# A two-layer hybrid backbone: z read behind the spill branch and gated on POOL, the latents' norm first, all z products ahead of the scans, and the second MoE's scale and shift on gathered rows

## The chip, the cores and the metric

The kernel runs on one core of one Trainium2 chip. A core has TensorE (PE in the profile, with its weight loads as PEld), VectorE (DVE), ScalarE (ACT), GpSimd (POOL) and SyncE (SP, which issues most DMAs here). Each engine works through its own queue of instructions in order. The metric is the device time of one execution in microseconds, the median of several runs.

## The reference

256 latent tokens and 256 context tokens of width 1024 go through two layers. Each layer has a mixer and a mixture of experts (MoE); each of these has its own norm, with scale, shift and gate from a conditioning vector. Layer 0 mixes by a gated convolution and differential attention, layer 1 ("odd") by a recurrent block. The layer-1 context is only needed up to its last scan state.

```python
h  = modulate(rms_norm(x, norm_mix[l]), sh1, sc1)        # h * (1 + scale) + shift
x  = x + g1 * mixer(h, hc)
hf = modulate(rms_norm(x, norm_ffn[l]), sh2, sc2)
x  = x + g2 * hier_moe(hf, ...)                          # the group's best, then two experts of its 4

# odd mixer, per direction (forward and reverse), u = second half of z = h @ w_in, y = gelu(first half)
uc = depthwise_conv(u, conv_w, conv_b)                   # four taps
r, i = sigmoid(block_diag(uc, w_a) + b_a), sigmoid(block_diag(uc, w_x) + b_x)
log_a = -8 * r * softplus(-lam)
a, b = exp(log_a), sqrt(-expm1(2 * log_a)) * (i * uc)
h_t = a_t * h_{t-1} + b_t                                # context first; the latents start from its end
y_lat = (y * (h_forward + h_backward)) @ w_out
```

Each token goes to 2 of 16 experts of width 512, and all is float32. The answer is the latent stream, 256 x 1024.

## The kernel before, in words

**Memory and order.** Working memory is 23 units of 128x2048 float32 (8 KB a partition) and some smaller pieces. Python code hands units out from one queue: `unit()` takes the one given back longest ago, `give()` puts one at the end. A weight tile of 1 MB fills a unit; the list `todo` holds the order of the weight loads, and `load_ahead(n)` keeps up to n loaded tiles ahead. So the place of a `give()` in the source sets which later tile or load gets that unit, and hence on whose work it waits. The source order gives the priority; the instructions are laid out on each engine by priority among those that a planner of the compiler holds to be ready, so their order isn't quite that of the source. `tc.issue_after(x)` puts an instruction behind x on its engine.

**Numbers.** Products that feed the routing are done with each operand as a high and a low part (`split`, L152: a copy on ACT, L155, and a subtraction, L158) in three matmuls (`mm3`, L176). MoE products use the operands as they are.

**First MoE (`moe0`, L1081).** The experts are done in four quarters of four. A quarter has 3 row blocks, in each of which every expert has 32 token rows. `four` (L1058) runs the four experts' 32-column products beside each other (L1066). The rows come by indirect DMA; the outputs of the first three quarters are scattered by indirect DMA into a DRAM tensor z with two places for each token (L1106). Rows of z that an over-full expert didn't write are zeroed by `empty()` in the second quarter, 8 indirect DMAs on POOL. The last quarter's outputs stay on chip and are added by one-hot products (`add`, L1234). Behind its up product, z is read by 8 DMAs on SP (L1213) into four units, the gate rows by two (L437); then comes `spill_rounds` (L973), a branch on the number of extra rounds, taken by all five engines (L980). Its body runs only when an expert got over 96 tokens (64 in layer 1), and the branch skipped it in these runs. Then POOL adds the two halves of z (L1223), DVE multiplies by the gate (L1224) and adds to the residual x (L1225), and `between` splits the first u weight (subtractions on DVE) and adds the first half of the last quarter: `add_gated` (L550: L554 times gate, L555 plus residual), squares and their sums on ACT (L1240).

**The odd mixer's norm (`second_T`, L516).** For the latents (s = 0), then the context (s = 1): the second half of the last quarter is added (`ready`), the root of the mean square is taken, x is normed (L529), transposed (L481), scaled (L544, L545) and split. Both `ready` calls come ahead of any transposes. `ada(1, 1)` (L366) makes the second MoE's scale and shift on PE (L391) among it.

**The odd mixer (`odd_mixer`, L1395).** Channels go in four groups i of 256. `z(i)`: split the weight u_i, 96 matmuls for both streams. `conv(i)`: a first tap on ACT (L1444), three on DVE (L1446), for both directions and halves. `gate(i)`: 8 matmuls (L1459), 8 sigmoids on ACT, a multiply on POOL (L1461). `tanhs`, `exps`, `roots`: on ACT by `table` (L1412), which chains all such calls in source order, since a change of function needs a table load (all L1415). `exps` has a step on DVE (L1476). `scan(i)`: multiply, scan, add (L1487, L1488, L1491). `yrows(i)`: the y product (L1499), `gelu`, `mix(i)` (L1508), and `outs(i)` (L1519), the output product. The order is written by hand (L1524 to L1574): z(3) comes behind scan(0) and scan(1).

**Second MoE (`moe1`, L1266).** `moe_norm` (L765) takes the logits from the raw residual by scaled router weights, and writes normed rows with scale and shift (L795, and L796 half on POOL); `in_parts` splits them (L158). `route` (L830) is a chain of some 45 small DVE operations; `rows_of` (L1048) makes one-hots S, and `gather` (L1285) picks rows by a product (L1293). Four quarters follow, with two row blocks.

Of the kernel before, what the change touches and what calls it, by code (L numbers as in the profile page):

```python
# [17 lines left out]
D = 1024  # L18
KD = 8
# [16 lines left out]
def backbone(ctx: ExitStack, tc: tile.TileContext, a: dict, out: bass.AP):  # L36
# [329 lines left out]
    def ada(l, g, late=False, tag="z"):  # L366
# [6 lines left out]
        def biases():  # L373
            r = piece([128, 512], "vectors")
            V.memset(r, 0.0)
# [140 lines left out]
    def second_T(ready, between):  # L516
# [5 lines left out]
        def over_rms(s, sq):  # L522
# [5 lines left out]
            for b in range(2):  # L528
                V.tensor_scalar(xn[:, b], xb(2 * s + b), r[:, b:b + 1], None, op0=ALU.mult)  # L529
            return xn  # L530

        for s in range(2):
            if s == 0:
                xn = over_rms(0, ready(0))
                sq = ready(1)
                between()
            else:
                xn = over_rms(1, sq)
                give(xt[1])
# [433 lines left out]
    def spill_rounds(l, cap, nb, load, key, w, nri):  # L973
# [6 lines left out]
        with tc.If(n > 0):  # L980
# [7 lines left out]
            V.memset(y, 0.0)  # L988
            cur = slot1.rearrange("p a b -> p (a b)")
            V.tensor_scalar(cur, slot0, float(cap), None, op0=ALU.add)  # L990
            with tc.For_i(0, n, 1):
                with tc.For_i(0, NE, 1) as e:
# [6 lines left out]
                    gather_slots(hgT, h2, Sl)  # L999
                    t = act_of(*[slots_by(hgT, [dyn(a[m][l, bass.ds(e, 1)])], KD, keep) for m in ("wg", "wu")])  # L1000
# [80 lines left out]
    def moe0(h2, ts, lg, rest, h2d):  # L1081
# [31 lines left out]
        def empty():  # L1113
# [6 lines left out]
            for i in range(2):  # L1120
                for b in range(NT):
                    scatter(rowi[:, i, b:b + 1], zero)
# [55 lines left out]
        for q in range(4):  # L1178
# [15 lines left out]
            if q == 1:  # L1194
                empty()
# [12 lines left out]
        zt = z.rearrange("(i b p) d -> i b p d", i=2, p=128)  # L1208
        zs = []
        for b in range(NT):  # L1210
            zs.append(unit([128, 2, D], "zb"))
            for i in range(2):
                nc.sync.dma_start(zs[b][:, i], zt[i, b])  # L1213
        gates = gate_rows(0, 5, 2)
        spill_rounds(0, CAP0, NT, again, key, w, nri)
# [6 lines left out]
        for b in range(NT):  # L1222
            G.tensor_add(zs[b][:, 0], zs[b][:, 0], zs[b][:, 1])  # L1223
            V.tensor_mul(zs[b][:, 0], zs[b][:, 0], gates[:, b // 2])  # L1224
            V.tensor_add(xb(b), xb(b), zs[b][:, 0])  # L1225
            give(zs[b])
# [7 lines left out]
        def add(h, b):  # L1234
# [4 lines left out]
            add_gated(b, h, p, gates[:, b // 2])  # L1239
# [17 lines left out]
        def ready(s):  # L1257
            for b in (2 * s, 2 * s + 1):
                add(1, b)
# [6 lines left out]
    def moe1(h2, ts, lg, rest):  # L1266
        nb = 2
        load_ahead(13)

        hp = [unit([128, 2, D], "hp", R) for _ in range(2)]  # L1270

        def in_parts(b):
            for i in range(2):
                c = slice(512 * i, 512 * i + 512)
                split(hp[0][:, b, c], hp[1][:, b, c], h2[b][:, c], V)

        in_parts(0)
        goh, ef, pos, key, w, nri = route(nb, lg, CAP1)
        rest()
        in_parts(1)  # L1280
        give(*ts)
        ks = view(small([128, 16], "ks"), [128, 2, nb])
        hgT = unit([128, KD, 256], "hgT")

        def gather(q):  # L1285
            S = piece([128, nb, 256], "S", R)
            rows_of(S, key, nb, q, range(NR1), ks)
            for k in range(0, KD, 2):
                p = bank([128, 2, 256])
                for i in range(2):  # L1290
                    for b in range(nb):
                        for m, h in enumerate(hp):
                            T.matmul(p[:, i], h[:, b, (k + i) * 128:(k + i + 1) * 128], S[:, b],  # L1293
                                     start=(b + m == 0), stop=(b + m == nb))
                evict(hgT[:, k:k + 2], p)

        gather(0)
# [26 lines left out]
        for q in range(4):  # L1324
# [15 lines left out]
            if q == 3:  # L1340
                spill_rounds(1, CAP1, nb, whole, key, w, nri)
# [53 lines left out]
    def odd_mixer(ready, wz):  # L1395
# [144 lines left out]
        exps(0)  # L1540
        exps(1)
# [151 lines left out]
```

## Time and profile before the change

| | us |
|---|---|
| median of 3 runs | 1043.9 |
| lowest and highest | 1042.34, 1045.82 |
| profiled execution | 1043.87 |
| its span in the profile | 1042.1 |

| engine | busy us | share of the span |
|---|---|---|
| PE | 953.0 | 91% |
| DVE | 430.3 | 41% |
| ACT | 282.0 | 27% |
| POOL | 133.3 | 13% |

The profile is of one execution. A line of a group has the source line, engine, operation and tile, then busy time, mean ns of one, and the idle time ahead of them with what ended it. A line of the timeline has start and length in us, the engine (SPq is SP's queue, PEldq PE's sequencer), the operation, and in brackets how long the engine was idle before it and for what. A busy PE can be a PE that runs at a lower clock: the granted clock stands beside it, 1.00 being full.

### The profile page before, as it was taken

The page shows a single profiled execution, that of the slowest core. Times are in us where ns is not written, and L with a number is a line of the kernel's source. Part 1 is how long each engine was busy: PE and PEld are TensorE (multiplying, and loading weights), DVE is VectorE, ACT ScalarE, POOL GpSimd, SP SyncE. Part 2 cuts the span into 40 slices and gives each one's busy share as a digit, 9 for nine tenths or more (in the row PEclk, how much of TensorE's full clock was granted, in tenths as well). Part 3 has the DMA queues.
Part 4 walks back from the last instruction along what each step waited for, and adds up shares of the span by engine and source line. Part 5 has one row for each costly group of instructions (what it writes and reads, how often), then busy time and mean ns, then how long its engine had stood idle before and what let it go on. Part 6 is the DMA issues. An engine that isn't in the chain of part 4 may idle for free. (4 is left out here: it accounts for less than half of the span.)

```text
span 1042.1 us, 16137 instructions
## 1 busy us (share of the span) xinstructions
PE 953.0 (91%) x6705; PEld 523.3 (50%) x6705; DVE 430.3 (41%) x946; ACT 282.0 (27%) x494; POOL 133.3 (13%) x117
## 2 busy tenths in 40 slices
PE   4699999999987999999999799995986899999987
PEld 2488756656876343343433246873644443434323
DVE  3756666666464020020101188748667321111102
ACT  3623333424121010010100036486862110001000
POOL 0254010121033211010010300212121000000000
PEclk9699999999997999999999899996997899999999
DMA  9932466779476699999999946220793499999994
GB/s 366 372 111 100 162 236 256 298 295 419 198 294 242 258 391 393 421 409 414 420 361 380 390 189 270 99 104 17 291 357 148 158 422 420 421 419 420 421 388 196
DMA packets 50705, 310.73 MB, mean 298 GB/s; under 512 B 8680, under 2 KB 9448, under 8 KB 16064
## 3 DMA queue, kind: packets, MB, share of 16 engines
q1 hardware_dynamic: 45648, 301.63, 72.9%
q0 software_dynamic: 4976, 7.99, 2.1%
q8 instruction: 55, 0.90, 0.3%
q14 instruction: 26, 0.21, 0.1%
HBM read 304.28 MB, written 13.70 MB: 305 GB/s over the span
## 5 line engine op out<-in xcount | busy, mean ns | idle before, releaser
L1066 PE MATMUL ba<-w,hgT 128*32 128x512 f32 x1536 | 181.3, 593 | 1.6 <-SPq L980 0.9
L1066 PEld LDWEIGHTS ba<-w,hgT 128*32 128x32 f32 x1536 | 55.7, 110 | 114.6 <-issue 109.2
L1066 PE MATMUL ba<-w,actT 128*32 128x512 f32 x800 | 95.2, 593 | 1.9 <-DVEq L980 1.1
L178 PE MATMUL bz<-hT,wsp 128*128 128x256 f32 (+1 forms) x224 | 77.6, 347 | 6.4 <-ACT wsp L155 6.4
L180 PE MATMUL bz<-hT,wsp 128*128 128x256 f32 (+1 forms) x224 | 75.2, 336 | 4.3 <-DVE wsp L158 4.3
L179 PE MATMUL bz<-hT,wsp 128*128 128x256 f32 (+1 forms) x224 | 75.2, 336 | 0.0
L1066 PEld LDWEIGHTS ba<-w,actT 128*32 128x32 f32 x800 | 33.9, 110 | 55.8 <-issue 50.8
L1066 PE MATMUL bz<-w,actT 128*32 128x512 f32 x480 | 56.0, 605 | 6.0 <-PEq L980 5.9
L1066 PE MATMUL bz<-w,hgT 128*32 128x512 f32 x512 | 60.5, 592 | 0.0
L155 ACT ACTIVATE wsp<-w 128x512 fp32r<-128x512 f32 (+1 forms) x60 | 42.7, 765 | 51.7 <-PE bz L180 18.0
L158 DVE TENSOR_TENSOR wsp<-w,wsp 128x512 fp32r<-128x512 f32 (+1 forms) x53 | 49.0, 958 | 10.3 <-ACT wsp L155 10.2
L178 PEld LDWEIGHTS bz<-hT,wsp 128*128 128x128 f32 x224 | 43.0, 192 | 15.3 <-ACT wsp L155 10.5
L180 PEld LDWEIGHTS bz<-hT,wsp 128*128 128x128 f32 x224 | 43.0, 192 | 9.8 <-DVE wsp L158 6.1
L179 PEld LDWEIGHTS bz<-hT,wsp 128*128 128x128 f32 x224 | 43.2, 193 | 3.0 <-issue 0.2
L1334 DVE SCALAR_TENSOR_TENSOR act<-ba,tg,silu 128x512 f32<-128x512 f32 x8 | 6.0, 751 | 90.1 <-PE ba L1066 90.1
L391 PE MATMUL bz<-w,sT 128*32 128x512 f32 x320 | 39.5, 612 | 3.8 <-DMA w<-in_ada_w_dram 3.8
L179 PE MATMUL bz<-wsp,hT 128*128 128x512 f32 x96 | 38.8, 405 | 3.4 <-DVE wsp L158 3.4
L1446 DVE SCALAR_TENSOR_TENSOR uc<-bz,ocw,uc 128x510 f32<-128x510 f32 (+2 forms) x48 | 34.4, 743 | 15.7 <-ACT uc L1444 15.1
L178 PE MATMUL bz<-wsp,hT 128*128 128x512 f32 x96 | 38.3, 405 | 2.4 <-ACT hT L155 2.4
L1461 POOL TENSOR_TENSOR uc<-uc,ii 128x512 f32<-128x512 f32 x16 | 25.8, 1626 | 104.4 <-ACT ii L1415 104.4
L1190 DVE SCALAR_TENSOR_TENSOR act<-ba,tg,silu 128x512 f32<-128x512 f32 x6 | 4.5, 752 | 83.5 <-PE ba L1066 83.5
L180 PE MATMUL bz<-wsp,hT 128*128 128x512 f32 x96 | 38.5, 401 | 0.0
(363 smaller groups left out, 1488.6 us busy)
## 6 DMA issues: line engine op xcount, KB each, us to landing
w<-in_wg_dram SPq DMA_DIRECT2D x64, 1024.0 KB, 12.2
w<-in_wu_dram SPq DMA_DIRECT2D x64, 1024.0 KB, 11.1
w<-in_wd_dram SPq DMA_DIRECT2D x64, 1024.0 KB, 10.7
w<-in_ada_w_dram SPq DMA_DIRECT2D x48, 1024.0 KB, 8.0
w<-in_od_w_in_dram SPq DMA_DIRECT2D x8, 1024.0 KB, 7.0
w<-in_w_qkv_dram SPq DMA_DIRECT2D x6, 1024.0 KB, 19.9
w<-in_w_conv_dram SPq DMA_DIRECT2D x6, 1024.0 KB
w<-in_ev_w_out_dram SPq DMA_DIRECT2D x4, 1024.0 KB
```

The lines of the kernel that those rows point to most:

```text
L155: S.activation(hi, src, AF.Copy)
L158: (eng or lo_engine()).tensor_sub(lo, src, hi.bitcast(F))
L178: T.matmul(o, l[0], r[0], start=start, stop=False)
L179: T.matmul(o, l[0], r[1], start=False, stop=False)
L180: final[0] = T.matmul(o, l[1], r[0], start=False, stop=stop)
L391: T.matmul(m[32 * j:32 * j + 32], sT[:, k], w[:, j * 512:(j + 1) * 512], start=(k == 0), stop=(k == KD - 1), tile_position=(0, 32 * j))
L1066: T.matmul(o[r][32 * j:32 * j + 32], rows(r, k0 + k)[:, 32 * j:32 * j + 32], ws[j][:, k], start=(k0 + k == 0), stop=(k0 + k == nk - 1), ti ...
L1190: V.scalar_tensor_tensor(act[r], u[r], tg[:, n:n + 1], sl[r], op0=ALU.mult, op1=ALU.mult)
L1334: V.scalar_tensor_tensor(act[r], u[r], tg[:, n:n + 1], sl[r], op0=ALU.mult, op1=ALU.mult)
L1446: V.scalar_tensor_tensor(c[:, :, j:256], src[:, :, 0:256 - j], tap, c[:, :, j:256], op0=ALU.mult, op1=ALU.add)
L1461: G.tensor_mul(uc[:, n], uc[:, n], ii)
```

## The change

1. **Order of loads.** u1, u2, u3 come first, then y0 to y3; before, y0 and y1 came between u2 and u3.
2. **z.** `empty` moves into the spill branch's body. The z reads (four of 1 MB) and the gate rows come behind the branch in the source, the gate rows first. z is multiplied by the gate on POOL. Its addition to x stays on DVE, behind the first half's gated adds, and its units are given back only there. The u weight is split with subtractions on POOL, behind those adds.
3. **The latents' norm first.** The context's gated adds of the second half are put behind the latents' last normed block on DVE.
4. **Order of the odd mixer.** z(3) and conv(3) come ahead of the scans.
5. **Second MoE.** The raw rows, divided by their root mean square, are gathered as two parts (a copy with scale on ACT, a difference on DVE), and scale and shift are applied per channel when the gathered, transposed rows are evicted. The tiles of scale and shift rows and the split go.

```diff
     for i in range(1, 4):
         w_rows(("u", i), a["od_w_in"][4 + i])
-        if i == 2:
-            for j in range(2):
-                w_rows(("y", j), a["od_w_in"][j])
-    for i in range(2, 4):
+    for i in range(4):
         w_rows(("y", i), a["od_w_in"][i])
...
-            V.memset(r, 0.0)
+            (G if late else V).memset(r, 0.0)
...
             if s == 0:
-                xn = over_rms(0, ready(0))
-                sq = ready(1)
+                xn, done = over_rms(0, ready(0))
+                sq = ready(1, done)
                 between()
...
-    def spill_rounds(l, cap, nb, load, key, w, nri):
+    def spill_rounds(l, cap, nb, load, key, w, nri, empty=lambda zeros: None, ab=None):
...
             V.memset(y, 0.0)
+            empty(y)
...
                     gather_slots(hgT, h2, Sl)
+                    for k in range(KD if ab else 0):
+                        V.tensor_scalar(hgT[:, k], hgT[:, k], ab[0][k], ab[1][k], op0=ALU.mult, op1=ALU.add)
...
-            if q == 1:
-                empty()
...
-        zt = z.rearrange("(i b p) d -> i b p d", i=2, p=128)
+        spill_rounds(0, CAP0, NT, again, key, w, nri, empty)
+        gates = gate_rows(0, 5, 2)
+        zt = z.rearrange("(i b p) d -> b p i d", i=2, p=128)
         zs = []
         for b in range(NT):
             zs.append(unit([128, 2, D], "zb"))
-            for i in range(2):
-                nc.sync.dma_start(zs[b][:, i], zt[i, b])
-        gates = gate_rows(0, 5, 2)
-        spill_rounds(0, CAP0, NT, again, key, w, nri)
+            nc.sync.dma_start(zs[b], zt[b])
...
             G.tensor_add(zs[b][:, 0], zs[b][:, 0], zs[b][:, 1])
-            V.tensor_mul(zs[b][:, 0], zs[b][:, 0], gates[:, b // 2])
-            V.tensor_add(xb(b), xb(b), zs[b][:, 0])
-            give(zs[b])
+            G.tensor_mul(zs[b][:, 0], zs[b][:, 0], gates[:, b // 2])
...
-            add_gated(b, h, p, gates[:, b // 2])
+            with tc.issue_after(after.ins) if after else nullcontext():
+                add_gated(b, h, p, gates[:, b // 2])
...
             if r == 0:
-                w = wtile(("u", 0))
-                wz.extend(split_cols(w, m, V) for m in range(2))
-                used(w)
                 for b in range(NT):
                     add(0, b)
+                for b in range(NT):
+                    V.tensor_add(xb(b), xb(b), zs[b][:, 0])
+                    give(zs[b])
+                    square(0, b)
+                w = wtile(("u", 0))
+                wz.extend(split_cols(w, m, G) for m in range(2))
+                used(w)
...
-        def ready(s):
+        def ready(s, after=None):
             for b in (2 * s, 2 * s + 1):
-                add(1, b)
+                add(1, b, after)
+                square(1, b)
```

The second MoE's gather, and the order of the odd mixer:

```diff
-                evict(hgT[:, k:k + 2], p)
+                V.tensor_scalar(hgT[:, k], p[:, 0], ab[0][k], ab[1][k], op0=ALU.mult, op1=ALU.add)
+                S.activation(hgT[:, k + 1], p[:, 1], AF.Identity, scale=ab[0][k + 1], bias=ab[1][k + 1])
...
-        load_ahead(13)
+        load_ahead(15)
...
         z(2)
+        conv(2)
         gate(1)
-        conv(2)
+        z(3)
+        give(*tiles[0], *tiles[1])
         tanhs(0)
         tanhs(1)
+        exps(0)
+        exps(1)
         gy = unit([128, KD, 256], "gy")
         mixT = unit([128, KD, 256], "mixT")
         yrows(0)
         yrows(1)
-        exps(0)
-        exps(1)
         roots(0)
         roots(1)
+        conv(3)
+        load_ahead(4)
         scan(0)
         scan(1)
-        z(3)
-        give(*tiles[0], *tiles[1])
         gelu(0)
         mix(0)
         mix(1)
         gate(2)
-        conv(3)
-        yrows(2)
         tanhs(2)
         exps(2)
+        yrows(2)
+        yrows(3)
+        give(whole)
         roots(2)
+        scan(2)
         gate(3)
         give(*wax)
-        yrows(3)
-        give(whole)
-        scan(2)
         tanhs(3)
...
-        step, *tokens = moe_norm(2, "a", *AB)
...
+            V.scalar_tensor_tensor(lg[:, b], lp, r, rc[:, 0], op0=ALU.mult, op1=ALU.add)
+            S.activation(hp[0][:, b], xb(b), AF.Copy, scale=r)
+
+            def low(b=b, r=r):
+                V.scalar_tensor_tensor(hp[1][:, b], xb(b), r, hp[0][:, b].bitcast(F), op0=ALU.mult, op1=ALU.subtract)
+
+            if b == 0:
+                low()
```

`low` of the second token block (b = 1) is handed to `gather(0)`, which issues it behind its one-hots.

More of the change, by code (lines that the diff above doesn't have):

```diff
@@ L1111, in scatter, with empty @@
             puts.append(st)
-        def empty():
+        def empty(zeros):
             row = small([128, 2, NT], "row")
@@ L1121, in empty @@
                 for b in range(NT):
-                    scatter(rowi[:, i, b:b + 1], zero)
+                    scatter(rowi[:, i, b:b + 1], zeros)
         def again():
@@ L1232, in put, with add @@
                 put_parts((yl[r][:, 0, hs], yl[r][:, 1, hs]), o[r])
-        def add(h, b):
+        def add(h, b, after=None):
             p = bank([128, 512])
@@ L1264, in moe0, with moe1, gather @@
         return ready, wz
-    def moe1(h2, ts, lg, rest):
+    def moe1(hp, lg, low):
         nb = 2
-        load_ahead(13)
[L1270 to L1277, printed above, removed]
+        load_ahead(15)
         goh, ef, pos, key, w, nri = route(nb, lg, CAP1)
-        rest()
-        in_parts(1)
-        give(*ts)
         ks = view(small([128, 16], "ks"), [128, 2, nb])
         hgT = unit([128, KD, 256], "hgT")
-        def gather(q):
-            S = piece([128, nb, 256], "S", R)
-            rows_of(S, key, nb, q, range(NR1), ks)
+        ab = [[t[1][:, 0, k:k + 1] for k in range(KD)] for t in (AT, BT)]
+        def gather(q, then=lambda: None):
+            S_ = piece([128, nb, 256], "S", R)
+            rows_of(S_, key, nb, q, range(NR1), ks)
+            then()
             for k in range(0, KD, 2):
@@ L1576, in odd_mixer @@
         g1 = gate_rows(1, 2, 1)
-        AB = moe_rows(1, 1), router(1, 1, "a")
+        parts = router(1, 1, "a")
+        hp = [unit([128, 2, D], "hp", R) for _ in range(2)]
         load_ahead(12)
-        step, *tokens = moe_norm(2, "a", *AB)
         outs(3, ((0, 0), (1, 0), (0, 1), (1, 1)))
@@ L1583, in odd_mixer @@
         load_ahead()
+        wa, rc = parts
+        lg = small([128, 2, 20], "lg")
+        sq = small([128, NT, 2], "sq_sums")
+        lows = []
         for b in range(2):
+            xT = []
+            lp = None
             for h in range(2):
                 add_gated(b, h, y[b][h], g1[:, 0])
-            step(b)
+                S.activation(piece([128, 512], "sq", BF), xb(b)[:, h * 512:(h + 1) * 512], AF.Square,
+                             accum_out=sq[:, b, h:h + 1])
+                p = bank([128, 4, 128])
+                for c in range(4):
+                    T.transpose(p[:, c], xb(b)[:, (4 * h + c) * 128:(4 * h + c + 1) * 128], ident)
+                xT.append(piece([128, 4, 128], "x2T"))
+                evict(xT[-1], p)
+            lp = bank([128, 20])
+            for c in range(KD):
+                T.matmul(lp, xT[c // 4][:, c % 4], wa[0][:, c], start=(c == 0), stop=(c == KD - 1))
+            ss = small([128, 1], f"ss{b}")
+            V.tensor_add(ss, sq[:, b, 0:1], sq[:, b, 1:2])
+            r = small([128, 1], f"rstd{b}")
+            rsqrt(r, ss, float(D), [128, 1], f"m{b}")
+            V.scalar_tensor_tensor(lg[:, b], lp, r, rc[:, 0], op0=ALU.mult, op1=ALU.add)
[4 more added lines that the diff above has]
+                low()
         give(g1)
-        return tokens
+        return hp, lg, low
     xT = first_norm()
```

20 lines of the change are left out of this document (10 added, 10 removed).

## The prediction

> **What bounds the kernel now.** I read the page first: its span and the rows of 40 slices, of 26 us each.
>
> ```profile
> span 1042.1 us, 16137 instructions
> PE   4699999999987999999999799995986899999987
> ...
> DMA  9932466779476699999999946220793499999994
> ```
>
> PE is busy nearly everywhere. The slices in which it isn't, after the start, are 22, 27, 29 and 30 (counted from 0): some 573 to 807 us. The DMA engines are full from slice 32 to the end but one, and have holes in the same stretch of 573 to 807 us. That is the second half of the first mixture of experts (MoE), the odd mixer, and the way into the second MoE. So I asked for busy times stage by stage there (columns: stretch, then its length; PE, weight loads, DVE, ACT, POOL; clock; DMA share; GB/s).
>
> ```profile
> 582.00:649.00 67.00, 57.98 (x428) 31.83 (x430) 42.32 (x75) 25.45 (x54) 9.06 (x6) 0.95 0.71 281
> 649.00:687.00 38.00, 38.00 (x235) 29.54 (x235) 27.83 (x44) 19.56 (x29) 8.73 (x7) 1.00 0.32 112
> 687.00:714.00 27.00, 23.37 (x121) 19.11 (x119) 12.95 (x18) 26.53 (x41) 1.84 (x2) 0.99 0.12 39
> 714.00:737.00 23.00, 14.25 (x60) 10.31 (x61) 20.27 (x26) 9.98 (x16) 6.47 (x3) 0.63 0.32 104
> 737.00:770.00 33.00, 32.73 (x107) 20.04 (x107) 22.74 (x27) 32.44 (x48) 8.73 (x5) 1.00 0.86 331
> 791.00:819.00 28.00, 14.51 (x98) 13.62 (x100) 22.15 (x95) 9.36 (x17) 2.85 (x2) 0.63 0.50 188
> ...
> 833.00:1010.00 177.00, 174.25 (x1444) 69.83 (x1437) 27.54 (x63) 16.46 (x28) 0.00 (x0) 1.00 1.01 421
> ```
>
> Each stage has its own limit. 649 to 687 is PE. 687 to 714 and 737 to 770 are ACT (26.5 of 27 and 32.4 of 33 us). 714 to 737 is nobody's: PE 14, ACT 10, DVE 20 of 23 us, a chain of waits. 791 to 819 is the chain of small DVE operations of the router. From 833 on it is the DMA: 1.01 at 421 GB/s, for the 96 weight tiles of 1 MB of the second MoE.
>
> The second MoE therefore decides how an earlier gain reaches the end. Its products start here:
>
> ```profile
> 818.74 14.80 PE L1066 MATMUL ba<-w,hgT 128*32 128x512 f32 x136
> ```
>
> By the code 23 units less five (residual, two parts of h, gathered rows, outputs) hold 18 tiles. They are full at 819, since the DMA did only 0.50 before; it goes on when PE frees the first four, two row blocks later, and is full from 833. If the first product comes X us earlier with 18 tiles ready, the DMA goes on X us earlier, and so does the end. I carry gains through one for one.
>
> **Step 1, 582 to 649: z, the gate and the norm.** First the branch and what z's reads do to it.
>
> ```profile
> L980 PEldq COMPARE_BRANCH  x2: 409/3258/6106, 581.7 to 1013.4; - x2
> 572.60 5.13 SPq L1213 DMA_DIRECT2D zb<-z  x8
> 588.89 2.35 POOL L1223 TENSOR_TENSOR zb<-zb 128x1024 f32<-128x1024 f32 x1 [1.04 <-DMA zb<-z]
> ```
>
> PE's sequencer hung 6.1 us in the first branch (581.7 to 587.8) and 0.4 us in the second. Around the first, SP's queue had z's 4 MB (572.6 to 577.7) and 1 MB of gates under way, and the last z tile came as the branch ended. One reading is that the branch waits for the traffic. The change puts the reads behind the branch in the source. But SP had passed its own branch before 572.6 here already, and the units that z now gets are those of the gathered rows, two of which the last up products read to their end; the gates' read now stands ahead of them in SP's queue. So the reads stay where they are or slip by some us, and much the same 5 MB are under way when PE branches. I take 0 for the branch; the ends are a gain of 5.7 us (6.1 less 0.4) and a loss of 4 (z as much later as the branch, and SP's weights for PE behind it). [...]
>
> Now DVE and POOL.
>
> ```profile
> L1224 DVE TENSOR_TENSOR zb<-zb,gates 128x1024 f32<-128x1024 f32 x4 | 4.7, 1218 | 0.0
> L158 DVE TENSOR_TENSOR wsp<-w,wsp 128x512 fp32r<-128x512 f32 x4 | 2.5, 691 | 0.1
> 616.19 0.60 ACT L892 ACTIVATE yl<-bz 128x512 fp32r<-128x512 f32 x1 [0.79 <-PE bz L1066]
> 621.09 1.29 DVE L893 TENSOR_TENSOR yl<-bz,yl 128x512 fp32r<-128x512 f32 x2
> 629.94 1.42 DVE L529 TENSOR_SCALAR xn<-xx,rstd 128x1024 f32<-128x1024 f32 x2
> 648.73 0.28 PE L180 MATMUL bz<-hT,wsp 128*128 128x256 f32 x1
> ```
>
> The gating of z (4 x 1.22 us) and the low parts of the first u weight (4 x 0.69) stand on DVE ahead of the first gated add: 7.6 us. The change gives both to POOL and puts the gated adds first. DVE is late here: the last expert part leaves ACT at 616.79, and its low half is done by DVE only at 622.38. Without the queue it is done at 616.79 + 0.69 = 617.5, so 4.9 us earlier; more than that PE doesn't allow. The latents' norm gains a further 2.75 us, as the context's four gated operations (4 x 0.69) now wait for its last multiply. Behind that wait stand all the context's operations, and the first z product needs both: the work on DVE from 617.5 to its end is the same, so its end at 649.0 moves by 4.9. I take 5 us of gain.
>
> POOL hides what it gets: its last add of z starts at 588.89; four multiplies of 2.35 end by 588.9 + 5 x 2.35 = 600.6, and four subtractions of half their size by 605.3. DVE needs the last z at 617.5 - 4.9 = 612.6, before its four adds, and PE the weight only behind the norm. The z units are freed later, which the ada weights used to wait for; they now take other units, freed by the last down products. Eight scatters of zeros leave POOL's queue in the second quarter, and a memset comes to it: 0, with POOL idle nearly all of those stages.
>
> **Step 2, 649 to 791: all z products ahead of the scans.**
>
> ```profile
> 713.25 1.06 ACT L1415 ACTIVATE gy<-gy 128x1024 f32<-128x1024 f32 x1
> 726.60 1.28 DVE L158 TENSOR_TENSOR wsp<-w,wsp 128x512 fp32r<-128x512 f32 x2
> 727.33 0.58 PE L180 MATMUL bz<-hT,wsp 128*128 128x256 f32 x1 [4.29 <-DVE wsp L158]
> 736.36 0.69 ACT L1415 ACTIVATE ii<-ba,ocw 128x512 f32<-128x512 f32 x1 [0.17 <-PE ba L1459]
> 768.02 2.19 ACT L1415 ACTIVATE b<-b 128x512 f32<-128x512 f32 x4
> 775.25 8.77 PE L1519 MATMUL bz<-w,mixT 128*128 128x512 f32 x16 [3.49 <-DVE mixT L1508]
> 784.27 7.13 PE L1519 MATMUL bz<-w,mixT 128*128 128x512 f32 x16
> L1415 ACT ACT_TABLE_LOAD x11 | 14.1, 1283 | 0.2
> L1444 ACT ACTIVATE uc<-bz,ocw 128x512 f32<-128x512 f32 x16 | 12.5, 780 | 30.7 <-DVE uc L1446 17.2 <-PE bz L180 13.5
> L1446 DVE SCALAR_TENSOR_TENSOR uc<-bz,ocw,uc 128x510 f32<-128x510 f32 (+2 forms) x48 | 34.4, 743 | 15.7 <-ACT uc L1444 15.1
> ```
>
> The fourth z product is the hole. Its weights are split into units that the first scans free, so the last parts come at 726.6, behind the scans on DVE; PE waits for them (4.3 us), and the third gate's last matmuls stand behind that product in PE's queue. ACT, done with the gelu at 714.31, has the gate's last sigmoid at 737.05: 22.7 us for a table load (1.28) and eight sigmoids (8 x 0.69 = 5.5), 6.8 us of work. With the product ahead of the scans, the split falls into DVE's idle time (13 of 27 us busy from 687 to 714), in units that the second product has long freed, and u3 is loaded ahead of y. PE had room for both y products and half of z(3) in its 23.4 us of 687 to 714; the other half (727.33 to the gate's last matmuls, under 9 us) joins them, from 5 us earlier, while ACT does its 26.5 us of tanh, exp and root. So the gate's first results are there when ACT comes. y0 and y1, now loaded behind u3, are wanted only after z(3). So 22.7 shrinks to 6.8: 15.9. Against it: conv(3)'s four first taps now lie in ACT's queue before that point, 4 x 0.78 = 3.1; two of u3's four high parts leave it, 0.6 each as half of the 1.28 that two low parts take on DVE, so 1.2. Net 14.0. The cover for conv(3)'s twelve DVE steps, 8.9 us, is the same idle time; if it fails, they delay the scans and 8.9 comes off, so the lower end is 5. The upper end is 16 + 1.6, as the 8.77 us product, at a clock that had fallen (7.13 the next time), could run at full clock. I take 14.
>
> After the gate ACT's chain is the same as before (tanh, exp, root, gate, tanh, exp, root: 736.36 to 770.21, with all its table loads), then scan, mix and two output products. It moves rigidly.
>
> **Step 3, 791 to 819: the second MoE's norm on gathered rows.**
>
> ```profile
> L795 DVE SCALAR_TENSOR_TENSOR h<-xx,rstd,AB 128x512 f32<-128x512 f32 x4 | 2.9, 746 | 0.0
> L158 DVE TENSOR_TENSOR hp<-h,hp 128x512 fp32r<-128x512 f32 x4 | 2.7, 686 | 0.1
> L796 DVE TENSOR_TENSOR h<-h,AB 128x512 f32<-128x512 f32 x2 | 1.4, 684 | 0.0
> L827 DVE TENSOR_TENSOR goh<-slot,gf 128x8 f32<-128x8 f32 x1 | 1.3, 1257 | 0.0
> ```
>
> DVE works without a pause between the last gated add and the gather's one-hots, so what leaves its queue counts in full: 4 x 0.75 + 4 x 0.69 + 2 x 0.68 = 7.1 us, and about 1.1 us that an 8-element step (L827, 1.26 instead of 0.16) waited beside POOL's half of the shift. Added: two low parts of 128x1024, at twice 0.75 each, 3.0 us; the second lies behind the one-hots and holds up the gather's last parts. Squares by halves save a little on ACT. The two row reads of scale and shift leave SP's queue, and the load limit goes from 13 to 15 tiles, while 18 units bound it as before: 0 for both. Net 7.1 + 1.1 - 3.0 = 5.2, and I take 6 with the squares. The ends are 2 and 9. The gather's evictions become one DVE and one ACT operation of 256 columns each per pair, beside each other; in the later quarters they lie under the down products: 0.
>
> **The sum.** 5 + 14 + 6 = 25 us. The profiled execution took 1043.87 us, 1.8 more than its span, and the median of the runs is 1043.9; so 1043.9 - 25 = 1018.9, and I say 1019.
>
> **Rivals.** *The scans keep waiting* (0.20): conv(3) runs on DVE ahead of the scans after all, and step 1 gives little, as the context's norm ends no earlier: 5 + 6 + 2 = 13, 1031. For it: DVE's queue is in order, and conv(3) waits for z(3). Against: 14 us of idle DVE.
>
> *More than that* (0.07): the branch falls to 0.4 us and every step reaches its upper end: 5 + 5.7 + 17.6 + 9 = 37, 1007.
>
> *DMA sets the end anyway* (0.05): 96 tiles at 421 GB/s are 239 us; if their start can't move, nothing does: 1044. Against: the DMA does 0.32, 0.12 and 0.32 from 649 to 737.
>
> *POOL holds up DVE* (0.06), the slower one.
>
> ```profile
> 719.92 5.07 POOL L1461 TENSOR_TENSOR uc<-uc,ii 128x512 f32<-128x512 f32 x2 [30.58 <-ACT ii L1415]
> 717.14 2.33 DVE L1488 TENSOR_TENSOR_SCAN uc<-rr,uc 128x512 f32<-128x512 f32 x2
> 720.58 3.36 DVE L1488 TENSOR_TENSOR_SCAN uc<-rr,uc 128x512 f32<-128x512 f32 x2
> 723.86 2.81 DVE L1491 TENSOR_TENSOR mixT<-uc 128x256 f32<-128x256 f32 x2
> 715.29 0.74 DVE L1491 TENSOR_TENSOR mixT<-uc 128x256 f32<-128x256 f32 x2
> ```
>
> Beside two POOL multiplies (2.5 us each) two scans took 1.0 and two adds 2.1 us longer: 1.55 us for each multiply. The gate multiplies now fall on the scans: 8 x 1.55 = 12.4, which leaves 14 - 12.4 = 1.6 of step 2. If POOL's z multiplies and subtractions also run at that pace (4 x 5.07 + 4 x 2.54 = 30.4) and DVE stands still for all of it, step 1 costs 30.4 - 7.6 = 22.8. Sum: 22.8 - 1.6 - 6 = 15 slower, 1059. It decides when DVE's stalls pass 25 us of these 43. Against: POOL is done with z before DVE is busy, by step 1. [...]
>
> **How the numbers follow.** My forecast, 13 to 35 us gained with 25 the likeliest, has 0.62. A measurement can tell about 0.3%, 3 us. Faster: 0.62 + 0.20 + 0.07 = 0.89; same: 0.05; slower: 0.06. The range leaves out the slower case, the unmoved one and the far end of the third: 1006 to 1033.
>
> **What would show it.** Right: xn of the latents by 623; z(3) on PE next to the second gate, with no wait for a split; one table load and eight sigmoids on end behind the first gelu; the last output product 19 us earlier; the first second-MoE product near 794, and the end 223 us after it. Wrong: scans with pieces of conv(3) ahead of them; DVE steps of over twice their length beside POOL; a PE branch of other than some 6 us; DMA below 1.0 between that first product plus 15 us and the last tiles.

## The result, and the profile after the change

| | before | changed |
|---|---|---|
| median us | 1043.5 | 1027.1 |
| lowest to highest | 1042.3 to 1045.8 | 1024.4 to 1028.7 |
| profiled span | 1042.1 | 1025.9 |

The ratio is 0.984, with a 95% interval of 0.983 to 0.986: 16.4 us faster, inside the range of 1006 to 1033, and 9 us short of the forecast of 25. From the page of the changed kernel, the span and the same rows of slices of 25.6 us as shown of before:

```profile
span 1025.9 us, 16145 instructions
...
PE   4699999999995999999999799998986999999987
...
DMA  9932456879657899999999785406584399999994
```

Behind 570 us PE's holes are those of before, and those in slices 27 and 31 have narrowed. Busy times by stage (stretch, length; PE, weight loads, DVE, ACT, POOL; clock; DMA share; GB/s):

```profile
576.00:644.00 68.00, 58.11 (x427) 31.53 (x430) 36.45 (x63) 21.45 (x48) 25.98 (x15) 0.95 0.74 288
644.00:684.50 40.50, 39.21 (x246) 30.16 (x240) 33.73 (x51) 25.99 (x41) 9.66 (x8) 1.00 0.27 105
684.50:714.00 29.50, 27.91 (x161) 23.64 (x159) 21.28 (x31) 27.46 (x42) 1.24 (x1) 1.00 0.48 163
714.00:722.00 8.00, 6.09 (x14) 3.21 (x15) 8.00 (x8) 6.57 (x10) 5.49 (x3) 0.79 0.50 189
722.00:758.10 36.10, 34.20 (x124) 20.45 (x122) 26.88 (x30) 34.38 (x48) 9.37 (x6) 1.00 0.68 254
...
778.20:802.60 24.40, 13.96 (x97) 13.26 (x96) 17.68 (x86) 9.73 (x19) 0.00 (x0) 0.65 0.34 130
818.00:994.00 176.00, 173.28 (x1432) 69.58 (x1425) 29.91 (x69) 18.90 (x33) 0.00 (x0) 1.00 1.01 421
```

The first stretch (branch to the end of z(0)) is no shorter: 68 us against 67. The stretch of 23 us behind the first gelu, which nobody filled (714 to 737 before), is now 8 us. The way into the second MoE is 24.4 us; from 818 on the DMA is full as before. The first product of the second MoE and the wait of PE's sequencer at the branch, from the timeline and from the waits:

```profile
802.57 1.92 PE L1066 MATMUL ba<-w,hgT 128*32 128x512 f32 x16
```

```profile
PE bz L1066 <- PEq L977: 6.6, 1, 6.6
```

From that product to the end it is 1025.9 - 802.6 = 223.3 us, against 1042.1 - 818.7 = 223.4 before. So the gain is all made ahead of it: 16.2 us in these two traces.

**Six of them were made ahead of the branch**, where nothing was forecast: the last transposes of the up product's result end at 575.0 instead of 581.1. The two timelines part in one place, the gate products of the first MoE's second quarter. Before, from 341 to 350 us:

```profile
341.39 1.03 PE L1066 MATMUL bz<-w,hg 128*32 128x512 f32 x7
342.61 1.06 PE L1066 MATMUL bz<-w,hg 128*32 128x512 f32 x4 [0.19 <-issue]
344.03 1.06 PE L1066 MATMUL bz<-w,hg 128*32 128x512 f32 x3 [0.36 <-issue]
345.45 4.35 PE L1066 MATMUL bz<-w,hg 128*32 128x512 f32 x17 [0.37 <-issue]
```

and the same product in the changed kernel:

```profile
340.69 3.62 PE L1066 MATMUL bz<-w,hg 128*32 128x512 f32 x32
```

One product of 32 matmuls took 8.3 us from its start to that of the next, instead of 3.4, a few matmuls every 1.4 us, with no semaphore to wait for ("issue"). In the kernel before, POOL issued the eight scatters of zeros just then (336.6 to 346.6 us). That suggested that the scatters, which the change took out of this quarter, had held up PE; the first runs test it.

### The profile page after: what moved, and what is told of

It reads as the page before. It is cut to its first block, busy times and chain, and to the rows that moved or that the text cites. A ratio compares the mean times of both kernels' runs of the same rounds, so it can differ in the third digit from the quotient of the medians.

```text
span 1025.9 us, 16145 instructions
## 1 busy us (share of the span) xinstructions
PE 947.8 (92%) x6705; PEld 514.7 (50%) x6705; DVE 425.8 (42%) x936; ACT 285.5 (28%) x504; POOL 137.8 (13%) x116
## 5 line engine op out<-in xcount | busy, mean ns | idle before, releaser
L1066 PE MATMUL ba<-w,hgT 128*32 128x512 f32 x1536 | 178.8, 593 | 1.5 <-DMA w<-in_wu_dram 1.5
L178 PE MATMUL bz<-hT,wsp 128*128 128x256 f32 (+1 forms) x224 | 77.0, 345 | 0.3 <-ACT hT L155 0.3
L180 PE MATMUL bz<-hT,wsp 128*128 128x256 f32 (+1 forms) x224 | 74.2, 333 | 0.0
L179 PE MATMUL bz<-hT,wsp 128*128 128x256 f32 (+1 forms) x224 | 74.2, 332 | 0.0
L1066 PE MATMUL bz<-w,hgT 128*32 128x512 f32 x512 | 58.0, 592 | 0.0
L178 PEld LDWEIGHTS bz<-hT,wsp 128*128 128x128 f32 x224 | 42.3, 189 | 7.3 <-ACT wsp L155 2.8
L180 PEld LDWEIGHTS bz<-hT,wsp 128*128 128x128 f32 x224 | 42.1, 189 | 4.8 <-issue 0.8
L179 PEld LDWEIGHTS bz<-hT,wsp 128*128 128x128 f32 x224 | 42.3, 189 | 4.3 <-DVE hT L158 0.8
L1066 PEld LDWEIGHTS bz<-w,actT 128*32 128x32 f32 x480 | 16.6, 112 | 42.8 <-issue 42.8
L1190 DVE SCALAR_TENSOR_TENSOR act<-ba,tg,silu 128x512 f32<-128x512 f32 x6 | 4.5, 751 | 78.4 <-PE ba L1066 78.4
```

What stands on the lines that cost most here:

```text
L178: T.matmul(o, l[0], r[0], start=start, stop=False)
L179: T.matmul(o, l[0], r[1], start=False, stop=False)
L180: final[0] = T.matmul(o, l[1], r[0], start=False, stop=stop)
L1066: T.matmul(o[r][32 * j:32 * j + 32], rows(r, k0 + k)[:, 32 * j:32 * j + 32], ws[j][:, k], start=(k0 + k == 0), stop=(k0 + k == nk - 1), ti ...
L1190: V.scalar_tensor_tensor(act[r], u[r], tg[:, n:n + 1], sl[r], op0=ALU.mult, op1=ALU.mult)
```

## The experiments

All comparisons below are on other chips than the first one; there the kernel before takes 1038.7 to 1039.6 us. Each line is the median, the median of before on the same chip, and the ratio with its interval.

| run | what | us | before | ratio |
|---|---|---|---|---|
| b1_after | the changed kernel | 1026.6 | 1039.4 | 0.988 (0.986 to 0.989) |
| a1_scatters_back | changed, scatters back | 1027.5 | 1039.4 | 0.988 (0.986 to 0.990) |
| a2_before_less_scatters | before, without the scatters | 1039.9 | 1039.4 | 1.000 (0.999 to 1.001) |
| a4_before_new_order | before, with the odd mixer's new order | 1029.0 | 1039.4 | 0.990 (0.988 to 0.992) |
| a3_after_old_order | changed, with the old order | 1037.8 | 1039.4 | 0.998 (0.997 to 0.999) |
| b2_after_old_norm | changed, with the old second-MoE norm | 1030.3 | 1039.4 | 0.992 (0.990 to 0.993) |
| c1_no_step1 | changed, without step 1 | 1025.5 | 1039.6 | 0.986 (0.984 to 0.988) |
| b3_no_order | changed, context not held back | 1026.8 | 1039.4 | 0.988 (0.986 to 0.989) |
| b4_u0_on_pool | b3, u0's high parts on POOL | 1032.8 | 1039.4 | 0.994 (0.992 to 0.995) |
| c2_conv_behind | changed, conv(3) behind the scans | 1031.2 | 1039.6 | 0.992 (0.990 to 0.993) |
| c3_conv_gelu | c2, gelu from PSUM | 1028.6 | 1039.6 | 0.990 (0.988 to 0.991) |
| d1_gelu_from_psum | changed, gelu from PSUM | 1024.1 | 1038.7 | 0.986 (0.984 to 0.988) |

### The scatters, and the changed kernel on another chip

```diff
+            if q == 1:
+                empty(zero)
...
-        spill_rounds(0, CAP0, NT, again, key, w, nri, empty)
+        spill_rounds(0, CAP0, NT, again, key, w, nri)
```

> The changed kernel, but with the eight scatters of zeros back in the second quarter of the first MoE, as before, instead of behind the spill branch. Theory 1: these scatters held up TensorE in the kernel before (its third gate product of that quarter took 8.3 us from 341.4, against 3.4 of the others), so taking them out is what brought the last up product 6 us earlier, and they are 6 of the 16.4 us gained. Then this kernel takes 5 to 6 us more than the changed one (1033), its DMA-issuing steps on POOL stand near 336 to 346 us, TensorE has gaps of some 1 us each there, and the last expert's products end near 579 again. Rival: the 6 us have another origin (order of the loads, units freed differently) and this kernel takes what the changed one does, 1027, within 1.5 us.

```diff
-            if q == 1:
-                empty()
```

> The kernel before, with the call that scatters eight rows of zeros left out and nothing else changed (no token of this input is past the capacity, so no row stays unwritten). Theory 1: 5 to 6 us less than the kernel before (1038), all of it gained by 350 us and carried to the end one for one. Rival, the scatters cost nothing by themselves: 1043.5 within 1.5 us. Rival, the lead is lost again at the branch, where z's reads and TensorE meet: under 3 us.

> The changed kernel itself, unaltered, beside the kernel before on the chip of the other runs of this call. On the chip of the first comparison the ratio was 0.984, but there the trace of before showed a gate product of 8.3 us (341.4 to 349.7) that no kernel since has shown, with the scatters or without. Theory 1b: that stretch, some 5 us, belongs to that chip and not to the kernel, and here the changed kernel is 11 to 13 us below the kernel before (ratio 0.987 to 0.990). Rival: the ratio is 0.984 here too, and the scatters' 6 us are part of the change's gain.

The scatters cost at most 1 us: with them the changed kernel takes 0.9 us more (the intervals overlap), and without them the kernel before takes the same. In the run of the new order alone, whose code up to there is that of before, the eight scatters lie at the same place and the product runs through:

```profile
342.06 3.62 PE L1063 MATMUL bz<-w,hg 128*32 128x512 f32 x32
```

So theory 1 falls, and with it what the first two expectations made of it (1033 and 1038). The changed kernel gains 12.8 us here (0.988), 3.6 less than on the first chip, where the kernel before is 4 us slower than on the four chips of the later runs and the changed one only 0.5. The 4.9 us that this one product lost (8.3 less 3.4) cover it in the trace. Why PE issued so slowly there stays open: from 343 to 345 us the DMA engines were as idle in the run that didn't stall (busy share 0.04, against 0.11), the changed kernel ran through on the first chip too, and no run made the stall come back. The kernel before itself wasn't profiled on a later chip, so that the stall is the first chip's own rests on its times there and on the kernels that share its code. With that, I count 12.8 us as the change's own gain.

### Step 2 alone and step 2 undone

The diff is the one of the odd mixer's order (z(3), conv(3), exps, scan(2), and u loaded ahead of y), put into the kernel before, and taken out of the changed one.

> The kernel before with only the odd mixer's new order (z(3) and conv(3) ahead of the scans, u loaded ahead of y). The prediction gave this step 14 us (1029.5). Theory 2, from the two traces: the gap between the kernels grows by 8 us from the end of z(0) to the end of the last output product, since the second gate's 15 us are paid back in part: the first gelu waits for the eviction of gy that now lies behind the scans' multiply in DVE's queue, and the third pair of output products runs at a fallen clock. Then this kernel takes 1034 to 1036. Rival: the order is worth its 14 to 15 us and the rest was lost elsewhere, 1029.

> The changed kernel with the odd mixer in its old order (z(3) and conv(3) between the gelu and the second half's scans, y0 and y1 loaded ahead of u2 and u3); everything else as changed. Theory 2 (the order is worth 8 us): 1035. Rival (it is worth 14): 1041. If the two kernels with one order each give different sizes, the order's worth hangs on step 1.

Step 2 is worth 10.4 us put in alone and 11.1 us taken out (between two chips; 10.7 by the ratios): nearly the same both ways, so it hardly leans on step 1. The 8 us of theory 2 are too few, and the forecast of 14 is too many. Where the rest is, ACT's timeline tells. Old order (the run of before without scatters), the first gelu and the last sigmoid of the second half's first gate:

```profile
707.80 1.06 ACT L1413 ACTIVATE gy<-gy 128x1024 f32<-128x1024 f32 x1
...
731.20 0.69 ACT L1413 ACTIVATE ii<-ba,ocw 128x512 f32<-128x512 f32 x1 [0.17 <-PE ba L1457]
```

New order alone, from the roots on (the two runs start this stage 1.0 us apart):

```profile
705.53 4.27 ACT L1412 ACTIVATE b<-b 128x512 f32<-128x512 f32 x8
711.68 1.28 ACT L1412 ACT_TABLE_LOAD   x1 [1.88 <-DVE gy L233]
712.97 1.06 ACT L1412 ACTIVATE gy<-gy 128x1024 f32<-128x1024 f32 x1
...
719.90 0.69 ACT L1412 ACTIVATE ii<-ba,ocw 128x512 f32<-128x512 f32 x1 [1.02 <-PE ba L1456]
721.60 0.69 ACT L1412 ACTIVATE rr<-ba,ocw 128x512 f32<-128x512 f32 x1 [1.02 <-PE ba L1456]
722.65 0.69 ACT L1412 ACTIVATE ii<-ba,ocw 128x512 f32<-128x512 f32 x1 [0.36 <-PE ba L1456]
```

From the gelu's end to the last sigmoid it was 731.89 - 708.86 = 23.0 us and is 723.34 - 714.03 = 9.3: 13.7 gained. But the gelu itself comes 714.03 - 708.86 - 1.0 = 4.2 us later. 1.9 of that is a wait for DVE's copy of gy, which DVE does only behind the first scan steps. And the sigmoids then wait 2.8 us for PE in all. (The spans of these two executions differ by 8.3 us, the medians by 10.9: a single execution is good to 1 or 2 us.)

### Where conv(3) belongs, and the gelu

In words: conv(3)'s steps on DVE are queued behind scan(1)'s last add, its first taps on ACT behind gate(2)'s last sigmoid.

```diff
-        conv(3)
         load_ahead(4)
...
         gate(2)
+        conv(3, scanned[-1], last[-1])
         tanhs(2)
```

> The changed kernel with conv(3) put behind the first half's scans on DVE, and its first taps behind the second gate's sigmoids on ACT; z(3) stays ahead of the scans. Theory 6, where the rest of step 2's 14 us is: conv(3)'s twelve steps are not covered; they and its four first taps bring roots, scans and the first gelu some 4 us later (714.0 in the run of the order alone, 708.9 in the old order, with 1 us between their starts), and the gelu waits on top of that for gy's eviction behind the scans' first multiply. With conv(3) behind the scans the gelu comes 3 to 4 us earlier, gate(3) doesn't suffer (its operands are wanted only 20 us later), and the time is 1022.5 to 1024. Rival: the gelu waits for TensorE's y products, and this is 1026 to 1027; or conv(3) now delays the second gate's scans, and it is slower than 1027.

```diff
-            evict(gy[:, 2 * i:2 * i + 2], o)
+            if i < 2:
+                yo.append(o)
...
+                for m, o in enumerate(yo):
+                    table(gy[:, 2 * m:2 * m + 2], o, AF.Gelu_apprx_tanh)
```

> As the run with conv(3) behind the scans, and the first gelu reads both y products from PSUM in two operations of 512 columns, without the copies of gy on ACT and DVE. Theory 6: the copies cost ACT one step of 0.6 us and make the gelu wait for DVE; 1 to 2 us less than with conv(3) behind the scans alone (1021 to 1023). Rival: the eviction is hidden and the banks held longer make the second gate wait: the same within 1 us, or slower.

> The changed kernel, with conv(3) where the change puts it (ahead of the scans, in DVE's idle time), and only this altered: the first gelu reads both y products from PSUM in two operations of 512 columns, so that the copies of gy on ACT (0.57) and on DVE (0.68) go. Theory 6, what is left of it after the runs that moved conv(3): the gelu's wait of 1.87 us for DVE's copy, which stands behind the scans' first multiplies, and ACT's copy are on the chain; without them the first gelu and the second gate come 2.4 us earlier, and the time is 1024 to 1025 (the changed kernel 1026.6 on this chip). Rival: the two banks held until the gelu make the second gate's products wait, as its last three sigmoids do already (1.8 us for TensorE), and nothing is gained: 1026 to 1027.5.

With conv(3) behind the scans it takes 4.6 us more, not 3 less. The table load ahead of the gelu shows the first reason, in the run with conv(3) moved and the copies still there:

```profile
712.96 1.28 ACT L1409 ACT_TABLE_LOAD   x1 [5.02 <-DVE gy L233]
```

The roots ended 2 us earlier, but DVE's copy of gy came only behind more scan steps. Without the copies (the second run) the gelu ends at 708.9 and the gate at 715.6, some 6 us earlier than in the changed kernel, and that is given back at once:

```profile
726.85 1.45 ACT L1441 ACTIVATE uc<-bz,ocw 128x512 f32<-128x512 f32 x2 [5.45 <-DVE uc L1444]
```

ACT stands 5.45 us ahead of conv(3)'s last two first taps, until DVE, behind its scans, has done the first half of conv(3). DVE was busy in each of the 20 us from 706 to 726. So of the two places tried, conv(3) is better where the change has it, with the copies (1026.6 against 1031.2) and without them (1024.1 against 1028.6): the half of theory 6 that blamed it falls, and the other half, the copy, stands. The run with only the copies gone takes 1024.1 us, 0.986 of before against 0.988 of the changed kernel. In its trace the gate ends 3.5 us earlier than in the changed kernel on a later chip (719.03 against 722.50), more than the 1.9 us of the wait:

```profile
710.17 1.28 ACT L1409 ACT_TABLE_LOAD   x1
711.47 1.08 ACT L1409 ACTIVATE gy<-ba 128x512 f32<-128x512 f32 x2
...
718.34 0.69 ACT L1409 ACTIVATE ii<-ba,ocw 128x512 f32<-128x512 f32 x1 [0.17 <-PE ba L1453]
```

The load follows the roots at once, and from the gelu's end (712.55) to the last sigmoid's (719.03) it is 6.5 us, close to the forecast's 6.8. PE's half of it, the last eight matmuls of that gate, in the changed kernel on a later chip and with the copies gone:

```profile
716.38 5.40 PE L1453 MATMUL ba<-uc,w 128*128 128x512 f32 x8 [3.30 <-ACT rr L1409]
```

```profile
714.60 3.70 PE L1453 MATMUL ba<-uc,w 128*128 128x512 f32 x8 [0.50 <-ACT rr L1409]
```

and the stretch of 718 to 722 us in each (the clock is the last figure but two), in the same order:

```profile
718.00:722.00 4.00, 4.00 (x7) 1.67 (x7) 4.00 (x4) 2.20 (x5) 4.00 (x3) 0.60 0.10 41
```

```profile
718.00:722.00 4.00, 4.00 (x19) 3.42 (x18) 4.00 (x3) 3.82 (x7) 4.00 (x3) 1.00 0.12 51
```

While ACT waited for the copy, PE waited 3.3 us for ACT to free its banks; the granted clock from 718 to 722 us was 0.60, and the eight matmuls took 5.40 us instead of 3.70 (with the order alone, also behind a wait of 3.30, 0.52 and 6.54). The last three sigmoids waited 1.8 us for PE, against 0.2 without the copies. The run without the copies has the lowest median of all, 2 to 2.5 us below the changed kernel by ratio and median, as its expectation had it, though the two ratios' intervals overlap a little, and by ratio the run without step 1 is as fast (0.986).

### Step 1

```diff
-                sq = ready(1, done)
+                sq = ready(1)
```

> The changed kernel without the one ordering that lets the context's gated adds start only after the last multiply of the latents' norm. Theory 3, why step 1 gave nothing at the end of z(0): with that ordering the latents' norm comes 4.5 us earlier, but the context's chain of root and multiply then finds DVE and ACT full of the latents' evictions (its square root ran 3.3 us after its input), its norm comes 4 us later, and z(0) needs both. Without the ordering, and with z's gating and u0's subtractions off DVE, the context's norm begins 4 us earlier and the latents' 2 us later; z(0) ends 2 to 4 us earlier, and 2 to 4 us come off the end (1023 to 1025). Rival: something else binds z(0) (the ada products between, the last expert part that leaves ACT late), and this is within 1 us of the changed kernel.

```diff
-                wz.extend(split_cols(w, m, G) for m in range(2))
+                wz.extend(split_cols(w, m, G, G) for m in range(2))
```

> As the run without that ordering, and u0's four high parts also copied by POOL instead of ACT. Theory 4: in the changed kernel the last expert part waits in ACT's queue behind u0's four copies and the squares (it leaves ACT 3.9 us after its product, 0.8 in the kernel before), so ACT's queue took the place of DVE's. With the copies off ACT the part leaves about 2 us earlier, and the norms and z(0) with it: 1 to 2 us less than without the ordering alone. Rival: POOL is too slow for copies and subtractions and u0 itself comes late (after 631), so it is the same or up to 5 us slower.

The third run takes all of step 1 out again (z's reads, gating on POOL, the latents' norm first).

> The changed kernel with all of step 1 undone: z read ahead of the branch, z's gating and u0's low parts on DVE, the context's gated adds not held behind the latents' norm; the eight scatters of zeros stay out (no token is past the capacity), and steps 2 and 3 stay. Theory 5: from 612 us to the last z product TensorE is the limit (33.6 of 36.7 us busy in the kernel before; only 3 us of holes), so an earlier norm is filled by waiting ada products and step 1 is worth 0 to 1 us, less what the gate's early matmuls put into z(1)'s way: this kernel takes 1025 to 1027.5, the changed one 1026.6. Forecast of the prediction: step 1 is worth 5, so this takes 1031 to 1032.

Step 1 is worth nothing: without it 0.986, with it 0.988, and the intervals overlap. Theory 5 expected that. Theory 3 falls: without the ordering nothing is gained. The context's chain was held back in the changed kernel, as its rows from the same chip show, 3.8 us between two small steps that need only a square root on ACT:

```profile
626.73 0.17 DVE L453 TENSOR_SCALAR rs_vx<-ss 128x2 f32<-128x2 f32 x1
...
630.72 0.16 DVE L455 RECIPROCAL rs_yx<-rs_yx 128x2 f32<-128x2 f32 x1
...
631.70 1.42 DVE L526 TENSOR_SCALAR xn<-xctx,rstd 128x1024 f32<-128x1024 f32 x2
```

Without the ordering the context's multiply starts at 625.4 instead of 631.7, and z(0) still ends at 644.5 (644.4 in the changed kernel). What binds is PE. Its busy time from the end of the first MoE's last down product to z(0)'s end, in the kernel before, with the new order alone, and in the changed kernel, the last two on the later chips:

```profile
616.10:649.00 32.90, 29.75 (x213) 20.84 (x216) 28.25 (x60) 20.38 (x45) 1.31 (x2) 1.00 0.82 330
```

```profile
612.50:645.40 32.90, 29.77 (x217) 20.83 (x216) 28.26 (x60) 20.34 (x45) 1.31 (x2) 1.00 0.82 332
```

```profile
612.40:644.40 32.00, 29.55 (x216) 20.49 (x216) 21.40 (x46) 15.97 (x37) 6.06 (x7) 1.00 0.59 231
```

Where step 1 isn't in, PE has 3.1 us of holes in 32.9, and that is all that an earlier norm can win. 48 ada matmuls stood between the last expert sums and the norm's transposes and filled the time while DVE was late; with the norm earlier, 24 of them come behind its first transposes. z(0) ends 0.9 us earlier (32.0 against 32.9), and then that is lost too: the first gate's matmuls, now ready earlier, stand among z(1), with a wait of 1.09 us for conv(0) on DVE ahead of four of them, and z(3) ends at 695.4 against 695.2.

The run with u0 on POOL answers theory 4 and shows the slow rival at work. DVE's adds of z's rows in it, POOL's step beside them, and DVE's adds in the run without it:

```profile
611.32 2.30 DVE L1248 TENSOR_TENSOR xx<-xx,zb 128x1024 f32<-128x1024 f32 x1
613.54 3.42 DVE L1248 TENSOR_TENSOR xctx<-xctx,zb 128x1024 f32<-128x1024 f32 x2
```

```profile
610.82 3.93 POOL L158 TENSOR_TENSOR wsp<-w,wsp 128x512 fp32r<-128x512 f32 x2
```

```profile
608.50 1.21 DVE L1248 TENSOR_TENSOR xx<-xx,zb 128x1024 f32<-128x1024 f32 x1
609.64 2.35 DVE L1248 TENSOR_TENSOR xctx<-xctx,zb 128x1024 f32<-128x1024 f32 x2
```

With its own copies POOL no longer waits for ACT's, so its subtractions fall on DVE's adds. The last three adds take 5.72 us of DVE instead of 3.56, the last is done at 617.0 instead of 612.0, the last expert part leaves ACT at 618.8 instead of 615.4, and the kernel is 6 us slower. Part of that is PE's clock: from 613.9 to 617.6 PE had a single matmul of 0.49 us, the granted clock from 617 to 621 was 0.50, and 21 matmuls of the last sums took 7.51 us, where 24 take 6.00 without. In the changed kernel the subtractions wait for ACT's copies and lie in a pause of DVE.

### Step 3

The diff is that of the second MoE's norm, gather and spill, taken out of the changed kernel.

> The changed kernel with the second MoE's norm as before (scale and shift on whole token rows, in DVE's queue; gathered rows evicted by one copy per pair of banks), all else as changed. The prediction gave this step 6 us (1033 beside 1027 for the changed kernel). From the two traces: from the last output product to the first product of the second MoE it went from 27.3 to 24.4 us, so 3 us: the low parts of 128x1024 (1.28 us each) both lie on the chain, and scale and shift in the evictions cost 0.6. Theory: 3 us more than the changed kernel. Rival: 6 us more, as forecast, with the trace's two stretches differing by something else.

It is worth 3.7 us, not 6: 27.9 us from the last output product to the first product of the second MoE, against 24.1 in the changed kernel on the same chip. What stands in the way, in the first trace of the changed kernel, from PE, DVE and ACT:

```profile
784.39 1.89 PE L1598 MATMUL ba<-wa,x2T 128*128 128x20 f32 x8 [1.47 <-DVE x2T L233]
```

```profile
787.48 1.28 DVE L1607 SCALAR_TENSOR_TENSOR hp<-xx,rstd,hp 128x1024 fp32r<-128x1024 f32 x1
```

```profile
798.38 0.56 ACT L1289 ACTIVATE hgT<-ba,BT,AT 128x256 f32<-128x256 f32 x1 [5.88 <-DVE hgT L1288]
799.87 0.56 ACT L1289 ACTIVATE hgT<-ba,BT,AT 128x256 f32<-128x256 f32 x1 [0.93 <-DVE hgT L1288]
```

The second block's logits wait for a transposed copy that stands behind the first low part on DVE. The second low part isn't behind the one-hots, as the source has it, but in the middle of the route. And the two halves of an eviction don't run beside each other: in all four pairs ACT's starts when DVE's ends, and its idle time ahead of it is put down to DVE's half (5.88 us, then 0.35 to 1.10 us behind the first pair). By the code both read one bank of PSUM; whether that is the reason was not shown, as no run gave the halves banks of their own. The stretch from the last one-hot to the first product grew from 6.4 to 7.0 us.

## Why the prediction was right or wrong, step by step

- **The carry-through** held: first product to end 223.3 us against 223.4, and 222.8 to 223.7 in every run. The DMA is full 15 us behind the first product.
- **The branch at 0** held: 5.9 us of PE before, 6.6 after. z's reads slipped, as expected, by some 8 us: SP issues them from 568.0 with z ahead of the branch (new order alone) and from 575.9 with z behind it (scatters back), and in both the DMA is all but full while PE waits, 5.7 us in each. So a backlog of reads didn't lengthen the wait in these two, but no run took the traffic away, and whether it makes it stays open. The kernels with the scatters inside the branch's body wait 6.4 to 7.2; why is not settled either.
- **Step 1, 5 us: wrong.** The step that failed is the sentence that the work on DVE to the context's norm is the same, "so its end at 649.0 moves by 4.9". The norm did come earlier (xn of the latents at 621.0, "by 623"), but z(0) hung on PE, which was busy 29.75 of the 32.9 us ahead of its end. I gave the stage to DVE because DVE was late, without adding up PE's queue: the ada products were there to be moved into the gap. A smaller slip: the last expert part waits in ACT's queue in place of DVE's (on the later chip it leaves ACT at 615.2, 2.8 us behind its product, 0.7 before). That wasn't shown to cost anything.
- **Step 2, 14 us: the mechanism was right, 10.4 to 11.1 by the runs.** Of its terms: 15.9 at the gate measured 13.7; the 1.9 by which ACT's own work brings the gelu later measured 4.2. The cover of conv(3), which I gave a lower end of 5, held. What the sum didn't have is DVE's copy of gy, an edit nobody made: scans and copy came to stand in DVE's queue in an order in which the copy is late, and the wait of 1.9 cost a further 2.8 at the gate with the order alone, and 1.4 and 1.8 in the two traces of the changed kernel, as PE's clock fell. With the copies gone the gate's stretch is 6.5, where 6.8 was forecast.
- **Step 3, 6 us: 3.7.** The terms taken off were real, but of the 8.2 us on DVE some had run while the second block's logits were on their way (DVE's L795 and the first parts, 795.6 to 800.1 of before), so they weren't on the chain. Both low parts that came in were (2 x 1.28), and the evictions cost 0.6 where I had 0.
- **The sum.** 10.4 to 11.1, 3.7, 0 to 1 for the scatters and -1 to 0 for step 1 make 13 to 16; together they measured 12.8. On the first chip the other 3.6 us came, as far as the traces show, from a stall of the kernel before that I had not looked at; it lies in slice 13 of the page, which reads 9 (my list of slices in which PE is not full also left out 11, 12 and 31, the last in the stretch I studied). All three terms of the forecast were too large, the first of them wholly. So the time came out nearer to the forecast than the three steps did, by luck: the 12.8 of the change itself are just under the 13 to 35 forecast, and are what the first rival (13, 1031) gives, though its mechanism didn't occur. Of the signs, the end came 223 us after the first product, as said, but the last output product came 13.2 us earlier, not 19, and the first product at 802.6, not 794.
- **The rivals.** The scans kept waiting: no, as DVE's idle time did cover conv(3). POOL holds up DVE: such a slowdown was measured (two scan multiplies, 1.28 us for both where POOL is idle, took 3.36 beside the gate's POOL multiplies), but in the changed kernel it hits steps that are not late (ACT, behind the gate, is busy 34.4 of the next 36.1 us); where a run put POOL's work beside DVE's adds of z, it cost 6 us.

## What to carry to other kernels

Before you credit a stage with an earlier start, add up the busy time of each engine from there to the stage's end: an engine that looks idle only because it waits may hold work that just changes places with the wait. When a reorder frees an engine, list what else sits in the queues that it passes, also small copies that no line of the diff names, and look for the idle gap that they make on PE: here 3.3 us of it were followed by a clock of 0.60. Look through the trace of before for stalls that no wait explains: a gain that comes from such a one may belong to the chip and not to the change.

## What the runs showed of the hardware

- Behind 3.3 us without a matmul the granted clock was 0.60 and 0.52 from 718 to 722 us, in two kernels; eight matmuls of 128x512 then took 5.40 and 6.54 us instead of 3.70. In the run with u0 on POOL, behind gaps of 1.08 and 2.15 us with one matmul of 0.49 us between them, it was 0.50 from 617 to 621 us.
- Beside POOL subtractions of 128x512 in the run with u0 on POOL, a DVE add of 128x1024 took up to 2.30 us, where it took 1.21 without them; the subtractions themselves took 1.97 us each, against 1.26 to 1.53 in the changed kernel.
- PE's wait at the branch was 5.7 us with z's 4 MB of reads issued 9 us ahead of it (new order alone) and 5.7 us with them issued 1 us ahead (scatters back). It was 5.7 to 5.9 in the five kernels with no scatters in the skipped body, and 6.4 to 7.2 in the nine with eight there.
- On one chip a product of 32 matmuls took 8.3 us instead of 3.4 with nothing in the trace to wait for; no trace of another chip showed it, nor that of the changed kernel on the same chip.
